# A hybrid decoder layer on one core: new order of the recurrence's levels, a steady weave with the output products, sixteen shared tiles, four PSUM banks in turn, and a weight column asked for sooner

## The chip, the core and the metric

The kernel runs on one core of one Trainium2 chip. A core has five engines that matter here: PE (TensorE, matrix products, with its weight loads shown as PEld), DVE (VectorE), ACT (ScalarE), POOL (GpSimd) and SP (SyncE, which here mostly starts transfers). Each engine executes its own instructions in order; semaphores tie the engines together. Data lies in HBM and is moved by DMA into SBUF (128 partitions); PE writes its sums into PSUM banks, from which ACT or DVE take them.

The metric is the device time of one execution in microseconds; the median of several runs is given.

## The reference

One layer of a decoder, 1024 tokens of width 1024 in float32, with 16 learned meta tokens ahead of them:

```python
h = h + 0.5 * swiglu(rms_norm(h, ffn1_norm[l]), ffn1_w_in[l], ffn1_w_out[l])
u = rms_norm(h, mix_norm[l]) @ w_in[l]
hq, hf, hi, hg, sq, sk, sv = jnp.split(u, ...)
o_hg = hgrn2(hq, hf, hi, hg, lb_all[l], hgrn_out_norm[l], valid)
o_sb = stick_breaking(sq, sk, sv, sb_q_norm[l], sb_k_norm[l], valid)
o = jnp.concatenate([o_hg, o_sb], axis=-1)
h = h + o @ w_out[l]
h = h + 0.5 * swiglu(rms_norm(h, ffn2_norm[l]), ffn2_w_in[l], ffn2_w_out[l])
```

The change lies in the middle: `hgrn2`, a gated linear recurrence of 4 heads (128 wide) over chunks of 128 tokens,

```python
bcum = jnp.cumsum(lf, axis=-2)
o_inter = jnp.einsum('bhtd,bhdv->bhtv', qk * jnp.exp(bcum), S)
attn = jnp.einsum('bhtd,bhsd,bhtsd->bhts', qk, kk, decay)      # decay = exp(bcum_t - bcum_s), causal
o_intra = jnp.einsum('bhts,bhsv->bhtv', attn, vk)
S_new = exp(b_last) * S + einsum('bhsd,bhsv->bhdv', kk * exp(b_last - bcum), vk)
```

then an RMS norm per head and a factor silu(g); `stick_breaking`, an attention of 8 heads; and the product with `w_out`.

## The kernel before

All large products are float32 by three products of split operands: a high part (rounded) and a low part of each side, `wh`, `wl` and `xh`, `xl`, added as xh·wh + xh·wl + xl·wh (lines 248 to 250). PE's instructions follow the order of the program text (`manual_schedule`), and that order is made by small planners: generators yield steps with a guess of their PE time in ns, and `weave` or `braid` deals them out. The other engines are ordered by a scheduler.

In order of time the layer is: the first feed-forward half (to about 760 us), the projections of the stick-breaking attention in four pairs of heads (`sb_project`, to about 843), the first of sixteen projected columns of the recurrence (`hgrn_fill`: v, f, q, g for each of 4 heads), the attention (`sb_jobs`) braided with these columns (to about 1160), the last columns beside the first steps of three heads, the recurrence (`hgrn_attend`) woven with the first half of the output product, `wo<-oT` (to 1293), the other half `wo<-oH` (to 1340), and the second feed-forward half.

**The passage from projections to attention.** `split_w` loads a column of weights (`raw`, 512 KB), casts its high part on ACT (line 231, kept as `self.rounded`) and takes the low part on DVE. `self.columns` is the list of columns asked for ahead; the last of it is the first column of the recurrence. `part` in `hgrn_fill` asks for column i+1 when column i begins. The pairs of `sb_project` end with `put_split`: q and k are scaled and split into `ohi` (ACT, line 1375) and `olo` (DVE, line 1376), in three buffers each, and stored to `qD` and `kD` by transfers that POOL starts (lines 1379 and 1380). For the last pair, p == 3, the splits are held behind `self.rounded` (line 1447), the newest cast at that time. The copies of the first projected column out of PSUM (`st`, line 1108) are held behind the cast of the column asked for last. The attention then loads `qs` and `ks`, makes its scores `z` (line 1599) and takes two sigmoids of each on ACT (`keep`, `sig`, lines 1605 and 1606).

**The recurrence.** `hgrn_attend` computes `attn` of a chunk level by level. After the diagonal (the `own` part, line 1199: products of KB and QA, masked with `ident` on DVE), each of the levels n = 1, 2, 4, ..., 64 takes: KP, a gathered copy of KB (ACT, line 1220); four products into a PSUM tile `lvl` (line 1225); the result put into `attn` (one `copy_predicated` on DVE up to n = 16, line 1232; copies on ACT above); then QA and KB are multiplied by the decays of the level (DVE, line 1255), which the next level reads. After the levels come the transposes of K (`knp`), the states (`s`, `up`), the outputs (`op`), their norm, a transpose (`onp`) and the split into `oH` (hi on ACT, lo on POOL). Before and between lie transposes of v (`flip`). Heads 0, 1 and 2 run as three streams, head 3 follows head 0.

PSUM has two banks for `lvl` (pool pz), two for `op` (po), two for small transposes (ptr) and two for projections.

`mix_out` is the output product: for each of 8 column blocks m and two halves of the tokens, four k steps of three products each; the first pass takes the attention's half of the rows (`oT`, k0 = 4), the second the recurrence's (`oH`, k0 = 0). `weave` runs a stream when its last step and the lag after it have passed, otherwise a step of the output product. The attention's result is read back from `oD` as `oT`, four tiles of 1 MB; the output weights come already split from `wout` in two buffers each.

## Time and profile before

| | |
|---|---|
| median of 3 runs | 1988.41 us (1987.54 to 1988.47) |
| the profiled execution | 1989.4 us |
| its span, first to last instruction | 1987.7 us |
| mean granted clock of TensorE | 0.998 |
| DVE, ACT, POOL busy | 1390.3, 854.7, 449.4 us |

The span is what the trace shows; the run's own time is 1.7 us longer, for what lies before the first and behind the last instruction. A row of a timeline gives start, duration, engine, line, operation, output and inputs, and in brackets how long the engine sat idle before it and what ended that. Lines with an L are those of the kernel before. One product of 4-byte operands shows as two records where it is 128 columns wide (a level's four products are eight records).

### The profile page before, as it was taken

How to read it: one execution, taken by the hardware profiler on the slowest of the kernel's cores; microseconds unless marked ns; L12 is line 12 of the kernel's file. 1: busy time of each engine (PE TensorE's matmuls, PEld its weight loads, DVE VectorE, ACT ScalarE, POOL GpSimd, SP SyncE). 2: the span in 40 equal slices, each digit the busy share in tenths (PEclk: the TensorE clock that was granted, in tenths of full speed). 3: DMA queues.
4: the chain of work that ended last, by engine and by line, in shares of the span. 5: the costliest groups of instructions: out<-in, count | busy, mean ns of one | idle time of the engine just before them, and what ended most of it. 6: DMA issues, size and time to landing. Idle time of an engine off the chain costs nothing.

```text
span 1987.7 us, 30439 instructions
## 1 busy us (share of the span) xinstructions
PE 1938.9 (98%) x10768; PEld 1631.7 (82%) x10768; DVE 1390.3 (70%) x2176; ACT 854.7 (43%) x1719; POOL 449.4 (23%) x616
## 2 busy tenths in 40 slices
PE   7999999999999999989999999899999999999998
PEld 6888888888888888878898978787888888888887
DVE  7977777877677765567777676567566766767774
ACT  6523443334444444456666635433233332344443
POOL 3010100010000003133333332220544544520000
PEclk9999999999999999999999999999999999999999
DMA  7366887758966225664454176665523323278463
GB/s 209 92 169 166 254 272 242 238 183 317 374 207 185 93 73 150 154 191 135 127 152 117 58 264 184 149 228 181 185 96 106 107 96 111 102 266 301 122 197 138
DMA packets 346168, 347.16 MB, mean 175 GB/s; under 512 B 94800, under 2 KB 250320, under 8 KB 346016
## 3 DMA queue, kind: packets, MB, share of 16 engines
q1 hardware_dynamic: 325168, 283.73, 46.5%
q0 software_dynamic: 19808, 61.49, 8.9%
q8 instruction: 85, 1.39, 0.3%
q14 instruction: 67, 0.55, 0.1%
q10 hardware_dynamic: 1040, 0.00, 0.0%
HBM read 233.75 MB, written 111.38 MB: 174 GB/s over the span
## 4 chain that ended last, share of the span: by engine, by line
PE 89%; DVE 4%; DMA 3%; ACT 2%; issue 1%; POOL 1%; SPq 0%; DVEq 0%; ACTq 0%; POOLq 0%
PE o L723 21%; PE qb L448 18%; PE qa L448 12%; PE qc L448 12%; PE proj L248 4%; PE proj L250 4%; PE proj L249 4%; PE flip L1454 2%; PE wo L248 1%; PE wo L249 1%; PE wo L250 1%; PE mq L992 1%; PE oacc L1529 1%; PE oacc L1531 1%; PE z L1599 1%
## 5 line engine op out<-in xcount | busy, mean ns | idle before, releaser
L448 PE MATMUL qb<-T,wh 128*128 128x512 f32 x1056 | 344.6, 390 | 1.4 <-ACT T L308 0.8
L448 PEld LDWEIGHTS qb<-T,wh 128*128 128x128 f32 x1056 | 198.1, 188 | 46.3 <-issue 2.5
L448 PE MATMUL qa<-B,wh 128*128 128x512 f32 x696 | 226.9, 391 | 0.0
L248 PE MATMUL proj<-xh,wh 128*128 128x512 f32 (+2 forms) x640 | 213.5, 334 | 2.6 <-ACT st L1108 1.5
L723 PE MATMUL o<-t,w 128*128 128x512 f32 x924 | 211.9, 390 | 0.5 <-DVE u L541 0.5
L250 PE MATMUL proj<-xl,wh 128*128 128x512 f32 (+2 forms) x640 | 209.8, 328 | 0.8 <-DVE xl L1918 0.8
L723 PE MATMUL o<-parts 128*128 128x512 f32 x924 | 209.9, 389 | 0.0
L249 PE MATMUL proj<-xh,wl 128*128 128x512 f32 (+2 forms) x640 | 209.7, 328 | 0.0
L448 PE MATMUL qb<-T,wl 128*128 128x512 f32 x528 | 205.4, 389 | 0.0
L723 PEld LDWEIGHTS o<-t,w 128*128 128x128 f32 x924 | 172.7, 188 | 37.4 <-issue 0.8
L723 PEld LDWEIGHTS o<-parts 128*128 128x128 f32 x924 | 173.3, 188 | 36.0
L361 DVE TENSOR_TENSOR wl<-s,wh 128x512 fp32r<-128x512 f32 x160 | 165.5, 1034 | 52.1 <-ACT wh L359 51.2
L359 ACT CAST wh<-s 128x512 fp32r<-128x512 f32 x160 | 99.4, 622 | 194.2 <-PE qb L448 150.7
L448 PEld LDWEIGHTS qa<-B,wh 128*128 128x128 f32 x696 | 130.8, 188 | 27.3 <-DVE B L827 0.3
L359 ACT CAST wh<-raw 128x512 fp32r<-128x512 f32 x120 | 74.4, 621 | 148.3 <-PE qc L448 106.6
L448 PE MATMUL qa<-B,wl 128*128 128x512 f32 x348 | 135.6, 390 | 0.0
L248 PEld LDWEIGHTS proj<-xh,wh 128*128 128x128 f32 x640 | 120.6, 188 | 14.7 <-ACT st L1108 1.7
L250 PEld LDWEIGHTS proj<-xl,wh 128*128 128x128 f32 x640 | 120.4, 188 | 12.2 <-DVE xl L1918 1.2
L249 PEld LDWEIGHTS proj<-xh,wl 128*128 128x128 f32 x640 | 120.5, 188 | 9.9
L448 PE MATMUL qc<-B,wh 128*128 128x512 f32 x352 | 115.0, 390 | 2.1 <-DVE u L541 2.1
L448 PE MATMUL qc<-T,wh 128*128 128x512 f32 x352 | 116.9, 394 | 0.0
L448 PEld LDWEIGHTS qb<-T,wl 128*128 128x128 f32 x528 | 99.1, 188 | 20.2
(398 smaller groups left out, 3871.8 us busy)
## 6 DMA issues: line engine op xcount, KB each, us to landing
raw<-in_ffn_w_in_dram SPq DMA_DIRECT2D x176, 256.0 KB, 4.0
raw<-in_ffn_w_out_dram SPq DMA_DIRECT2D x112, 256.0 KB, 4.3
w2in<-both SPq DMA_DIRECT2D x28, 512.0 KB, 3.4
raw<-in_w_in_dram SPq DMA_DIRECT2D x25, 512.0 KB, 4.8
ks<-kD SPq DMA_DIRECT2D x32, 260.0 KB, 5.0
wout<-both SPq DMA_DIRECT2D x16, 512.0 KB, 4.0
wh<-w2in SPq DMA_DIRECT2D x27, 256.0 KB, 3.2
wl<-w2in SPq DMA_DIRECT2D x27, 256.0 KB, 3.4
```

Of the source, the lines that this page charges most:

```text
L248: nc.tensor.matmul(ps, wh[:, s], xs, start=k == 0, stop=False)
L249: nc.tensor.matmul(ps, wl[:, s], xs, start=False, stop=False)
L250: nc.tensor.matmul(ps, wh[:, s], xl[:, k, c0 : c0 + n], start=False, stop=k == nk - 1)
L359: nc.scalar.copy(hi, src)
L361: nc.vector.tensor_sub(lo, src, hi.bitcast(F32))
L448: nc.tensor.matmul(ps, a[:, k, :], b[:, k, :], start=start and k == 0 and i == 0, stop=k == 3 and i == 2, skip_group_check=True,)
L723: nc.tensor.matmul(banks[bank][m], y[:, m * P : (m + 1) * P], z, start=start and at == 0 and e == 0, stop=q == nq - 1 and e == 2, skip_gro ...
L992: nc.tensor.matmul(ps[at : at + 32, at_g, :], self.xm[:, 4 * h + k, :], got[i, h][:, k, :], start=h == 0 and kk == 0, stop=h == 1 and kk = ...
L1454: self.nc.tensor.transpose(ps[:m, j, :], src[:, s0 : s0 + m], self.ident)
L1529: nc.tensor.matmul(o[:, c], vj, w[0], start=j == 0, stop=False, skip_group_check=True)
L1531: nc.tensor.matmul(o[:64, c], vj[:, :64], w[1], start=False, stop=end, skip_group_check=True)
L1599: nc.tensor.matmul(z, q, ks[0][:, s0 : s0 + n], start=True, stop=False)
```

## The change

Five things are changed.

1. The list of columns asked for ahead ends with the first two columns of the recurrence instead of one; the first column's turn may ask for one more. The splits of the last pair are held behind the cast of the second column instead of the newest one, and so are the copies of the first projected column.
2. A level multiplies KB by its decay right behind KP's copy, and QA right behind the products, ahead of `copy_predicated`. In the own part QA is multiplied ahead of the masking.
3. The tiles `lvl` and `op` take four PSUM banks in turn (`level_bank`: z and o alternate, two buffers each).
4. `weave` has a mode `steady`: a step of the output product comes whenever its share of planned time is behind that of the streams. The lags are changed (levels 6500 to 1500, own part 3200 to 1700, others), a step may carry a third number, its weight, and the last k steps are kept for the end.
5. `oT` is in 16 tiles of 128x512 (256 KB), eight for each half of the tokens, and their first asking comes behind the first weights; the last store of g is held behind them. The output weights of the second half use the same 16 slots (`w_tags`). Head 3's low part of oH is taken on DVE instead of POOL.

The diff, cut to its core:

```diff
+class Blocks:
+    def __init__(self, tiles):
+        self.tiles, self.shape = tiles, (P, len(tiles), 512)
+
+    def __getitem__(self, at):
+        rows, k, cols = at
+        return self.tiles[k][rows, cols]
...
+            for i, tag in enumerate(self.w_tags):
+                t = self.wp.tile([P, n], F32R, tag=tag, name="w" + "hl"[i], bufs=self.w_bufs)
+                self.last_load = nc.sync.dma_start(t.bitcast(F32), parts[:, i])
                 got.append(t)
             return got
...
                 nc.vector.tensor_mul(t, t, ps)
-            nc.sync.dma_start(dst[kind][h, :, s], t)
...
+            store = lambda: nc.sync.dma_start(dst[kind][h, :, s], t)
+            if (kind, h) == plan[-1] and c0 == HALVES[1][0]:
+                self.stores.append(store)
+            else:
+                store()
...
         def part(i, ci, c0, n, half):
             if ci == 0 and half == 0:
-                kept["w"] = kept["next"] or self.ahead_w.pop(cols[0])
-                kept["next"] = weights(i + 1) if i + 1 < len(plan) else None
-                kept["round"] = self.rounded.ins
+                kept["w"] = self.ahead_w.pop(cols[i])
+                for c in cols[i + 1 : i + (3 if i == 0 else 2)]:
+                    if c not in self.ahead_w:
+                        self.ahead_w[c] = self.col_tile(self.a["w_in"][0], c)
+                kept["round"] = self.rounds[cols[1]]
...
+    def level_bank(self, shape, name):
+        self.level_banks = self.level_banks[::-1]
+        tag = self.level_banks[0]
+        return (self.pz if tag == "z" else self.po).tile(shape, F32, tag=tag, name=name)
...
+        own = []
         for half in range(2):
-            ps = self.pz.tile([P, 4, P], F32, tag="z", name="lvl")
+            own.append(self.level_bank([P, 4, P], "lvl"))
             for j in range(4):
                 c = slice((4 * half + j) * P, (4 * half + j + 1) * P)
-                nc.tensor.matmul(ps[:, j, :], KB[:, c], QA[:, c], start=True, stop=True)
+                nc.tensor.matmul(own[half][:, j, :], KB[:, c], QA[:, c], start=True, stop=True)
+        nc.vector.tensor_mul(QA, QA, F)
+        for half, ps in enumerate(own):
             m = self.ident.unsqueeze(1).broadcast_to([P, 4, P])
             nc.vector.tensor_mul(attn[half], ps, m)
-        nc.vector.tensor_mul(QA, QA, F)
         tm = FM
...
-        yield 1740, 3200
...
-            ps = self.pz.tile([P, 2, 4, P // 2], F32, tag="z", name="lvl")
+            ps = self.level_bank([P, 2, 4, P // 2], "lvl")
             kp = pool.tile([P, 4 * P], F32, tag="KP", name="KP", bufs=2)
             nc.scalar.copy(
                 kp.rearrange("p (b h r) -> p b h r", h=2, r=n),
                 strided(KB, 0, (2 * n, 4 * nb), (512 + n, 2), (1, n)),
             )
+            decayed(KB, 0, 512 + n, 1, 8 * nb - 1)
             for c in range(4):
...
+            decayed(QA, n, 512 - n, 0, 8 * nb + 1)
             if n <= 16:
...
         for i, n in enumerate(LEVELS):
             level(i, n)
-            nb = 512 // (2 * n)
-            for eng, x, x0, x1, t0, t1 in (
-                (nc.vector, QA, n, 512 - n, 0, 2 * nb + 1),
-                (nc.vector, KB, 0, 512 + n, 1, 2 * nb - 1),
-            ):
-                y = strided(x, x0, (x1, 2), (2 * n, nb), (1, n))
-                eng.tensor_mul(y, y, strided(decays[i], t0, (t1, 2), (2, nb), (0, n)))
-            yield 890, 6500
+            yield 890, 1500, 2350 if n <= 16 else 1380
...
-        yield 1740, 4500
+        yield 1740, 2500, 5000 if last else 2800
...
-            ps = self.po.tile([P, 4, P], F32, tag="o", name="op")
+            ps = self.level_bank([P, 4, P], "op")
...
-            yield 1740, 3000
+            yield 1740, 3000, 9000 if last and half else 1740
...
+            eng = nc.vector if last else nc.gpsimd
+            eng.tensor_sub(lo[:, h, :], t, hi[:, h, :].bitcast(F32))
+            yield 430, 0, 2500 if last and half else 430
...
-            self.columns.append(self.columns_of_heads()[0])
+            self.columns += self.columns_of_heads()[:2]
...
-            with self.tc.issue_after(self.rounded.ins) if p == 3 else ExitStack():
+            with self.tc.issue_after(self.rounds[self.columns[-1]]) if p == 3 else ExitStack():
                 self.put_split(to, p, slice(c0, c0 + n), t[:, :n], mix, gain)
...
+                kept["w"] = ws.pop(m) if m in ws else self.rows_tile(k0, m)
+                if not k0:
+                    ws[m] = kept["w"]
...
-            self.product(ps, ws[m], *o[half], 0, n, [k])
+            self.product(ps, kept["w"], *o[half], 0, n, [k])
...
-    def weave(self, fill, streams=(), total=0.0, work=0.0, brief=False):
+    def weave(self, fill, streams=(), total=0.0, work=0.0, brief=False, steady=False):
...
             even = not work or spent * work <= (done + 6000) * total
-            if not ready and filling and join is None and (even or not live):
+            behind = steady and spent * work <= done * total
+            if filling and join is None and (behind or not ready and (even or not live)):
...
                 clock += step[0]
-                done += step[0]
+                done += step[-1] if len(step) == 3 else step[0]
...
                     def from_dram(half):
-                        got = []
-                        for i in range(2):
-                            t = self.pool_o.tile([P, 4, 512], F32R, name=f"oT{half}{i}")
-                            nc.sync.dma_start(
-                                t.bitcast(F32),
-                                oD[:, :, i, 512 * half : 512 * half + 512]
-                                .rearrange("k p t -> p k t"),
-                            )
-                            got.append(t)
-                        return got
+                        got = [[], []]
+                        for k in range(4):
+                            for i in range(2):
+                                t = self.pool_o.tile([P, 512], F32R, tag="o", name="oT", bufs=16)
+                                with tc.issue_after(self.last_load.ins) if half else ExitStack():
+                                    self.last_oT = nc.sync.dma_start(
+                                        t.bitcast(F32), oD[k, :, i, 512 * half : 512 * half + 512]
+                                    )
+                                got[i].append(t)
+                        return [Blocks(x) for x in got]
 
                     def first_half_of_o():
+                        ws = {0: self.rows_tile(4, 0)}
                         o = [from_dram(0)]
-                        yield 5000.0
+                        for store in self.stores:
+                            with tc.issue_after(self.last_oT.ins):
+                                store()
...
-                        self.weave(first_half_of_o(), lanes, 64 * 650.0 + 5000.0, 4 * 15900.0)
+                        self.weave(first_half_of_o(), lanes, 64 * 650.0 + 4000.0, 114850.0, steady=True)
...
-                    self.weights("wo2", 2, KT, c1)
+                    self.wp, self.w_tags, self.w_bufs = self.pool_o, ("o", "o"), 16
```

How this moves instructions, at three places. First ACT, around the splits of the last pair (`ohi`). Before, from the f column's sigmoids (L1114, L1115) on:

```order
L1114 ACTIVATE st<-proj 128x264
L1115 ACTIVATE st<-proj 128x264
L231 CAST wh<-raw 128x1024
L1375 ACTIVATE ohi<-qT,qg_82 128x512
L1114 ACTIVATE st<-proj 128x256
L1115 ACTIVATE st<-proj 128x256
L1375 ACTIVATE ohi<-qT,qg_82 128x512
L1114 ACTIVATE st<-proj 128x256
L1115 ACTIVATE st<-proj 128x256
L1375 ACTIVATE ohi<-kT,kg 128x512
L231 CAST wh<-raw 128x1024
L1375 ACTIVATE ohi<-kT,kg 128x528
```

and now, from the copies of the normalisation (`sbo`) on:

```order
L1455 COPY sbo<-sbs 32x65 x4
L1119 COPY st<-proj 128x264
L1459 ACTIVATE sbs<-sbs,eps 128x65
L1400 ACTIVATE ohi<-qT,qg_82 128x512
L1119 COPY st<-proj 128x256
L1400 ACTIVATE ohi<-qT,qg_82 128x512
L1400 ACTIVATE ohi<-kT,kg 128x512
L1119 COPY st<-proj 128x256
L1421 CAST vhl<-vt 128x32
L1400 ACTIVATE ohi<-kT,kg 128x528
L241 CAST wh<-raw 128x1024
L1125 ACT_TABLE_LOAD
```

Before, the splits stood behind the cast `wh` of a later column and among the f column's sigmoids; now all four stand ahead of that cast, of the table load and of the sigmoids.

Second PE, from the last projected column to the first output products. Before:

```order
L1225 MATMUL lvl<-QA,KP 128x2x64 x4
L1199 MATMUL lvl<-QA,KB 128x128 x8
L1454 MATMUL flip<-ident,vT 16x128
L1454 MATMUL flip<-ident,vT 128x128 x4
L1225 MATMUL lvl<-QA,KP 128x2x64 x2
L1454 MATMUL flip<-ident,vT 128x128 x4
L1225 MATMUL lvl<-QA,KP 128x2x64 x6
L1199 MATMUL lvl<-QA,KB 128x128 x8
L1225 MATMUL lvl<-QA,KP 128x2x64 x12
L248 MATMUL wo<-oT_12775,wh 128x512
L249 MATMUL wo<-oT_12775,wl 128x512
L250 MATMUL wo<-oT_12777,wh 128x512
```

and now:

```order
L1254 MATMUL lvl<-QA,KP 128x2x64 x4
L1219 MATMUL lvl<-QA,KB 128x128 x8
L1254 MATMUL lvl<-QA,KP 128x2x64 x4
L1479 MATMUL flip<-ident,vT 16x128
L1479 MATMUL flip<-ident,vT 128x128 x8
L1254 MATMUL lvl<-QA,KP 128x2x64 x4
L258 MATMUL wo<-oT,wh 128x512
L259 MATMUL wo<-oT,wl 128x512
L260 MATMUL wo<-oT,wh 128x512
L1254 MATMUL lvl<-QA,KP 128x2x64 x4
```

Before, six groups of levels and two own parts stood ahead of the first `wo`, which then ran 21 products at once; now three groups and one own part do, and behind the third group one or two k steps (of three products each) stand between any two levels. In all, from the last projection to the first product with `oH`, the output products stood in 25 runs before and stand in 42 now.

Third DVE, in the levels of three heads. Before:

```order
L1232 COPY_PREDICATED attn<-wide,lvl 128x2x64x4
L1255 TENSOR_TENSOR QA<-QA,Ts 128x2x64x4
L1255 TENSOR_TENSOR KB<-KB,Ts 128x2x64x4
L1232 COPY_PREDICATED attn<-wide,lvl 128x2x128x2
L1255 TENSOR_TENSOR QA<-QA,Ts 128x2x128x2
L1255 TENSOR_TENSOR KB<-KB,Ts 128x2x128x2
```

and now:

```order
L1241 TENSOR_TENSOR KB<-KB,Ts 128x2x32x8
L1241 TENSOR_TENSOR QA<-QA,Ts 128x2x128x2
L1262 COPY_PREDICATED attn<-wide,lvl 128x2x128x2
L1241 TENSOR_TENSOR KB<-KB,Ts 128x2x64x4
L1241 TENSOR_TENSOR QA<-QA,Ts 128x2x32x8
L1262 COPY_PREDICATED attn<-wide,lvl 128x2x32x8
```

Before, a level was copy, QA, KB; now KB of the coming level, QA of the one whose products have just run, and its copy behind them.

At the end of the recurrence two k steps stood between the last `op` and `onp`, and two behind; now four stand ahead of `onp`, and the products with `oH` follow it at once.

39 lines of the change are left out of this document (22 added, 17 removed).

## The prediction

> **What bounds the kernel now.** I read the page first, then busy time by stretch (windows), then the table of what PE waited for in each stretch, and last the timelines around those waits. The page's busy shares and the chain that ended last:
>
> ```profile
> PE 1938.9 (98%) x10768; PEld 1631.7 (82%) x10768; DVE 1390.3 (70%) x2176; ACT 854.7 (43%) x1719; POOL 449.4 (23%) x616
> PE 89%; DVE 4%; DMA 3%; ACT 2%; issue 1%; POOL 1%; SPq 0%; DVEq 0%; ACTq 0%; POOLq 0%
> ```
>
> PE is busy 1938.9 of 1987.7 us. The change takes no product away, so all it can win is PE's idle time, 48.8 us over the whole program, and time at a low clock. The windows of the places that the diff touches (stretch, length, then busy us and count of PE, PEld, DVE, ACT, POOL, then granted clock, DMA share, GB/s):
>
> ```profile
> 843.00:846.00 3.00, 1.51 (x13) 1.30 (x12) 1.29 (x3) 1.96 (x5) 1.63 (x2) 1.00 0.05 18
> 866.00:871.00 5.00, 0.00 (x0) 0.00 (x0) 2.00 (x2) 1.39 (x3) 0.54 (x1) 0.95 1.05 338
> 871.00:877.00 6.00, 5.17 (x14) 3.38 (x15) 4.49 (x6) 4.50 (x12) 3.14 (x9) 0.50 1.03 324
> 1162.00:1172.00 10.00, 9.32 (x61) 8.13 (x60) 5.30 (x8) 2.82 (x6) 8.58 (x25) 1.00 0.98 384
> 1170.50:1213.40 42.90, 37.87 (x252) 32.89 (x251) 40.76 (x61) 18.84 (x36) 12.87 (x30) 1.00 0.70 214
> 1213.40:1250.00 36.60, 35.14 (x260) 31.57 (x259) 21.61 (x49) 20.75 (x70) 12.05 (x20) 1.00 0.60 166
> 1250.00:1293.50 43.50, 38.97 (x235) 32.75 (x234) 21.23 (x39) 18.08 (x55) 11.97 (x12) 1.00 0.68 164
> ```
>
> The first three rows are the passage from the projections to the attention: PE does nothing from 866 to 871, and the six microseconds behind that run at a clock of 0.50. The last three are the recurrence beside the first half of the output product. PE idles 5.0, 1.5 and 4.5 us there, 11.0 together. In the first of them DVE is busy 40.76 of 42.90 us, in the other two only about half the time: its 83.6 us of work for these 123.0 us are crowded into the front. What PE waited for, in the passage and in the recurrence (us in total, times, longest; three rows of 0.4 us and less left off):
>
> ```profile
> PE z L1599 <- ACT sig L1606: 6.5, 4, 5.6
> PE proj L248 <- ACT st L1108: 1.5, 1, 1.5
> ```
>
> ```profile
> PE onp L1314 <- DVE vT L1308: 2.5, 2, 1.6
> PE lvl L1199 <- DVE attn L1232: 2.0, 3, 0.8
> PE lvl L1225 <- DVE QA L1255: 1.7, 3, 0.8
> PE lvl L1225 <- ACT KP L1220: 1.5, 2, 0.9
> PE wo L248 <- DMA wh<-wout: 1.1, 1, 1.1
> PE lvl L1225 <- DVE attn L1232: 0.9, 2, 0.5
> PE flip L1454 <- ACT vr L1188: 0.7, 1, 0.7
> PE lvl L1225 <- DVE attn L1201: 0.5, 1, 0.5
> ```
>
> The eight rows make 10.9 us, with the three left off 11.7 from 1160 on. Nothing else in the diff meets a wait of PE.
>
> **Part 1: the second column asked for sooner.** Why PE stood still, in the timelines of SP, POOL, ACT, DVE and PE (start, duration, instruction, idle before it and its releaser), and the transfer times of the first split stores of the pair before (tile ohi, 810 to 820) and of the last pair's (tile olo, 855 to 872):
>
> ```profile
> 831.39 0.62 SPq L226 DMA_DIRECT2D raw<-in_w_in_dram  x1
> 844.37 4.13 POOL L1438 TENSOR_TENSOR nat<-nat,sbs 128x512 f32<-128x512 f32 x4 [23.69 <-DVE sbs L1435]
> 853.89 1.28 ACT L1114 ACT_TABLE_LOAD   x1 [2.57 <-PE proj L250]
> 857.41 1.05 ACT L231 CAST wh<-raw 128x1024 fp32r<-128x1024 f32 x1
> 858.34 0.73 ACT L1375 ACTIVATE ohi<-qT,qg 128x512 fp32r<-128x512 f32 x1
> 870.21 0.77 DVE L1376 SCALAR_TENSOR_TENSOR olo<-kT,kg,ohi 128x528 fp32r<-128x528 f32 x1 [2.37 <-DMA qD<-olo]
> 871.07 0.29 ACT L1606 ACTIVATE sig<-z 128x144 f32<-128x144 f32 x1 [3.68 <-DVE olo L1376]
> 871.42 0.75 PE L1599 MATMUL z<-ks,qs 128*128 128x456 f32 x1 [5.58 <-ACT sig L1606]
> 877.46 0.39 PE L1454 MATMUL flip<-ident,sig 128*128 128x128 f32 x2
> DMA to landing us min/median/max: 2.8/4.1/6.1
> DMA to landing us min/median/max: 6.7/8.0/8.8
> ```
>
> The chain, backwards: z waits for ACT's sig, which stands in ACT's order behind the last split of k; its second half (olo, 870.21) waited for the landing of a qD<-olo store whose buffer it reuses. That store was slow (6.7 to 8.8 us, against 2.8 to 6.1 for a pair before) because the splits of the last pair ran at 858.34 and later, beside loads of the attention. And they ran there because L1447 holds them behind the cast of the newest column asked for, the one at 857.41.
>
> Now two columns are on the early list: the second is loaded right behind the first (near 822 by SP's listing, ten microseconds before 831.39), and the splits are held behind its cast. By ACT's order that cast stands right behind the copies of qT, so it runs near 838 (estimate from the ACT work listed ahead of it). The splits can then follow the normalised tiles, from about 848 (844.37 + 4.13 = 848.5 is the end of POOL's products), ten microseconds sooner and before the attention's loads. What this takes away: the 5.58 us gap; the 1.49 us wait of proj on ACT st (the 1.5 in the table), since the copies st stood behind the second column's cast and now do not; and the low clock in the burst of six z groups from 871.42 to 877.46 (6.0 us). At full clock this burst goes by ACT's pairs of keep and sig: 4.50 us of ACT work in the row 871 to 877, so I take 4.8 us, 1.2 less.
>
> What it adds: ACT has the four splits, the third column's cast and the table load now ahead of the first sigmoids, where the splits were behind them. The last splits need a buffer of which the store must land: first store about 850.2, landed 853.0 to 856.3 (2.8 to 6.1), then split 0.73, cast 1.05, table load 1.28, two sigmoids near 0.4 each: 856.9 to 860.2. PE, ahead by the 1.49 us, wants that PSUM bank from about 855. So a new wait of 1.9 us at the quick end, up to 5 at the slow one; I take 2.2, near the quick end, because these stores now meet little other traffic (the row 843 to 846 has a DMA share of 0.05). Sum of part 1: 1.49 + 5.58 + 1.2 - 2.2 = **6.1 us**, from 3.3 (new wait 5) to 8.3 (no new wait).
>
> The row 871 to 877 is what the Trainium skill describes in "TensorE: Matmul & The Clock Gate", section "HAM oscillation — how this bites in real kernels": an idle of some 3.4 us halves the clock. The trace agrees, with 5.58 us idle and then 0.50. By that rule a new wait above 3.4 us would halve the clock behind 855 too, so part 1 at its slow end would come to about 0 in place of 3.3.
>
> **Part 2: levels, banks and steady weave.** No product goes or comes; the prices of the pieces (DVE groups in 1160 to 1300; PE starts):
>
> ```profile
> L1232 DVE COPY_PREDICATED attn<-wide,lvl 128x512 f32<-128x512 uint8 x20 | 19.0, 952 | 10.6 <-PE lvl L1225 10.6
> L1255 DVE TENSOR_TENSOR QA<-QA,Ts 128x512 f32<-128x512 f32 x24 | 16.7, 696 | 5.8 <-PE lvl L1225 5.6
> L1255 DVE TENSOR_TENSOR KB<-KB,Ts 128x512 f32<-128x512 f32 x24 | 16.1, 687 | 0.8 <-ACT KP L1220 0.8
> 1170.53 1.07 PE L1225 MATMUL lvl<-QA,KP 128*128 128x128 f32 x8
> 1171.44 1.05 PE L1199 MATMUL lvl<-QA,KB 128*128 128x128 f32 x8
> 1184.97 0.48 PE L248 MATMUL wo<-oT,wh 128*128 128x512 f32 x1
> 1185.29 0.39 PE L249 MATMUL wo<-oT,wl 128*128 128x512 f32 x1
> 1185.52 0.40 PE L250 MATMUL wo<-oT,wh 128*128 128x512 f32 x1
> DMA to landing us min/median/max: 7.2/9.4/11.6
> ```
>
> A level of one head costs PE 0.91 us (1170.53 to 1171.44) and DVE 0.95 + 0.70 + 0.69 = 2.3. Before, levels of three heads stood behind each other and PE waited for DVE between them; 21 output products then ran at once. Now one or two k steps of wo (three products of 0.23, 0.69 us) stand between levels: 0.91 + 1.5 x 0.69 = 1.9 us of PE for 2.3 of DVE, instead of 0.91. The eight waits, one by one. The longest onp wait (1.6) has four wo steps, 2.8 us, ahead of it instead of two: gone, 0.4 of the 2.5 left. Own products behind attn, 2.0: four banks in turn instead of two, 0.5 left. QA, 1.7: its product now comes ahead of copy_predicated, but DVE still paces the levels, 1.0 left. KP, 1.5: KB's product no longer queues behind copy_predicated and QA on DVE, 0.5 left. The 1.4 behind attn: 0.5 left. flip and the rows left off, 0.7 + 0.8: 1.0 left. wo on DMA, 1.1: see below, 1.0 left. 11.7 becomes 4.9, a gain of 6.8. Against it: the first wo product behind small products takes 0.32 us to the next start (1184.97 to 1185.29) where the others take 0.23, so a switch costs 0.09; the listing has 42 runs of wo among the small products instead of 25, 17 x 0.09 = 1.5 us. Sum of part 2: 6.8 - 1.5 = **5.3 us**. At most 11.7 - 1.5 = 10.2; at the other end the 2.3 - 1.9 = 0.4 us by which DVE is short at each of the 20 levels with a copy_predicated comes back as waits, 8 us, which with 1.5 leaves 11.7 - 9.5 - 1.2 (the waits of wo and flip that stay) = 1.
>
> The tiles of oT: eight of 256 KB instead of two of 1 MB, all asked for once the first output weights are, behind the last proj (about 1170.7). 2.0 MB and 0.5 MB of weights at the 384 GB/s of row 1162 to 1172 take 6.8 us; the first k needs 1.0 MB, landed near 1175, the last near 1180. PE's new order has three level groups, an own group and nine flips (some 6 us) ahead of the first wo, and reaches the four k steps between 1177 and 1181: just in time, 0 to 2 us short, 1.0 taken above. Before, the first wo could start only at 1184.97.
>
> The Trainium skill speaks against such a split: "DMA: Bandwidth & Descriptors", section "Measured (HBM→SBUF, 128 partitions, SWDGE, issued from GpSimd)", has 1 MB as the size from which a transfer reaches three quarters of the peak, 64 KB at 32%. The row 1162 to 1172, with transfers of 256 and 512 KB queued behind each other, moves 384 GB/s and does not bear this out; by the page at, say, half the rate the last k would land near 1187, which is the late case among the rivals.
>
> At no cost: head 3's subtraction on DVE instead of POOL (0.69 by the QA row; nine output products, 2.1 us, run ahead of its reader), and the second set of output weights in oT's slots (half of it is loaded while half a pass of wo is left; the rest is asked for 11 us before its products, more than the 9.4 us in the landing row). Without that cover the first costs 0.7, the second 1 to 2.
>
> **Sum.** 1987.7 - 6.1 - 5.3 = 1976.3 us of span. The profiled run was 1989.4, its span 1987.7 and the median of the runs 1988.41, so a median stands 0.7 above a span: **1977.0**.
>
> **Rivals.** (a) Only part 1 pays; DVE paces the recurrence either way. For it: DVE's 40.76 of 42.90, and 2.3 against 1.9 per level. Against it: the slack of DVE behind 1213 into which the weave spreads it. 1988.4 - 6.1 = 1982.3. (b) Only part 2 pays: the wait moves to 855, 5 us long, and the clock halves there. For it: the row 871 to 877, and the 6.1 us at worst for a store. 1988.4 - 5.3 = 1983.1. (c) Slower: oT's tiles come late. They queue one behind the other, and the old ones took 7.2 to 11.6 us; PE executes in order, so a wo product waiting at 1177 holds every level behind it. It decides from a stall of about 5 us, the fourth k landing behind 1186: then 6 us idle, the clock at 0.50 for six more (3 us lost, as at 871), and 5.3 us of part 2 not won since DVE stands still meanwhile and is the pacing engine afterwards. 1988.4 - 6.1 + 6 + 3 = 1991.3. Against it: 384 GB/s in that row. (d) The change does not do what it says: the sooner load or cast finds no buffer and the splits stay late, and the levels keep their waits: 1988.4.
>
> **Chances.** Both parts pay: 0.62, and the time is that case's, 1977.0, with its own range 1970 (8.3 + 10.2) to 1983 (3.3 + 2.1). (a) 0.15, (b) 0.09, (c) 0.09, (d) 0.05. The range for 8 of 10 reaches over (a) and (b): 1969 to 1985.5. Of this kernel a measurement can tell 0.2%, 4 us, from no change, so faster means below 1984.4: all of the forecast's 0.62 but 0.01, 0.11 of (a) and 0.06 of (b), 0.78 in all. Same: 0.04 of (a), 0.03 of (b), 0.01 of the forecast, 0.01 of (c), 0.04 of (d), 0.13. Slower: 0.08 of (c), 0.01 of (d), 0.09.
>
> **What would show it.** Right in part 1: ohi on ACT near 848, the qD stores landing in under 6 us, no PE gap above 1 us between 860 and 880, clock 1.00 there, and one new PE wait near 855 on ACT st of about 2 us. Wrong: that wait above 3.4 us with a low clock behind it. Right in part 2: PE idle of about 5 us in the recurrence instead of 11.0, the first wo near 1177, DVE's busy share nearly even over its thirds, no onp wait above 0.5. Wrong: rows of lvl waiting for DVE that sum to more than 6 us, or wo waiting for oT. Anything that differs behind 1340, or before 800, is in no term here.

## The result

| | before | after |
|---|---|---|
| median of 6 runs | 1988.47 us (1987.54 to 1989.32) | 1974.95 us (1973.41 to 1976.45) |
| profiled execution, its span | 1989.4, 1987.7 us | 1973.63, 1971.9 us |
| mean granted clock | 0.998 | 0.999 |

The ratio after to before is 0.9932, 95% interval 0.9919 to 0.9945: 13.5 us faster, where the prediction's 1977.0 stood for 11.4. The two profiled executions lie on the far sides of their medians, so their spans differ by more, 15.8 us, and what follows from these two traces has to be read with that in mind. Where that came from, by the start of the same product in both traces:

| from ... to | before | after | won |
|---|---|---|---|
| start to the first projected product (`proj`) | 697.17 | 696.84 | 0.33 |
| ... to the first product of the attention's output (`oacc`) | 882.73 | 875.16 | 7.24 |
| ... to the last projection's first of three products | 1169.84 | 1161.24 | 1.03 |
| ... to the first product with `oH` | 1293.72 | 1278.46 | 6.66 |
| ... to the second feed-forward half's first product | 1340.01 | 1323.96 | 0.79 |
| ... to the last product | 1981.77 | 1965.82 | -0.10 |

Rows two and three are part 1 and what hangs on it, row four is part 2: the kernel with part 1 alone, among the experiments below, has 178.31, 286.08 and 123.79 us for the three stretches, where the kernel before has 185.56, 287.11 and 123.88. Row five is not explained in full: one wait of 0.33 us for a weight (`wl`) is gone, but the kernel with part 1 alone already has 45.69 of the 46.29 us there.

**The passage after.** What PE waited for from 840 to 885, and the windows of these microseconds (columns as before):

```profile
PE proj L258 <- ACT st L1126: 1.3, 1, 1.3
PE z L1624 <- ACT sig L1631: 1.1, 4, 0.5
```

```profile
843.00:846.00 3.00, 3.00 (x28) 3.00 (x27) 0.80 (x2) 1.51 (x6) 0.66 (x1) 1.00 0.86 162
846.00:853.00 7.00, 7.00 (x60) 7.00 (x60) 5.06 (x8) 3.57 (x8) 6.66 (x10) 1.00 0.39 137
853.00:857.00 4.00, 2.72 (x22) 2.51 (x21) 2.82 (x5) 3.15 (x5) 1.26 (x5) 1.00 0.95 336
857.00:864.00 7.00, 7.00 (x54) 6.65 (x53) 1.03 (x3) 1.99 (x4) 0.00 (x0) 1.00 0.76 228
864.00:871.00 7.00, 6.16 (x30) 4.02 (x29) 6.46 (x10) 6.73 (x21) 2.63 (x5) 1.00 0.68 188
```

The 8.0 us of waits of before are 2.4, PE works from 846 to 853 without a break, and the clock stays at 1.00. The one new wait of any size stands where it was expected. ACT ahead of it, PE behind it, and the transfer times of the last pair's stores (tiles ohi and olo, 845 to 870):

```profile
847.17 0.72 ACT L1400 ACTIVATE ohi<-qT,qg 128x512 fp32r<-128x512 f32 x1 [2.58 <-DVE qT L1469]
852.24 0.74 ACT L1400 ACTIVATE ohi<-kT,kg 128x528 fp32r<-128x528 f32 x1 [1.95 <-DMA qD<-ohi]
852.88 1.03 ACT L241 CAST wh<-raw 128x1024 fp32r<-128x1024 f32 x1
853.93 1.28 ACT L1125 ACT_TABLE_LOAD   x1
855.95 0.39 PE L258 MATMUL proj<-xh,wh 128*128 128x256 f32 x1 [1.28 <-ACT st L1126]
DMA to landing us min/median/max: 2.7/3.4/3.8
DMA to landing us min/median/max: 2.8/3.5/4.1
```

The first split runs at 847.17 instead of 858.34. The fourth waits 1.95 us for a store to land, then come the cast and the table load, and PE gets its bank 1.28 us late.

**The recurrence after.** What PE waited for from 1160 to 1280, and the windows of the recurrence:

```profile
PE knp L1290 <- DVE kms L1284: 1.6, 3, 0.6
PE wo L258 <- DMA oT<-oD: 0.9, 2, 0.5
PE lvl L1254 <- DVE QA L1220: 0.8, 1, 0.8
PE flip L1479 <- ACT vr L1207: 0.7, 1, 0.7
PE lvl L1254 <- DVE QA L1241: 0.6, 1, 0.6
PE flip L1479 <- DMA vT<-hg_v: 0.3, 1, 0.3
PE wo L260 <- DMA oT<-oD: 0.2, 1, 0.2
```

```profile
1161.90:1180.00 18.10, 16.36 (x106) 13.21 (x105) 17.24 (x25) 6.93 (x11) 10.87 (x29) 1.00 0.84 261
1180.00:1220.00 40.00, 38.97 (x268) 34.05 (x268) 27.60 (x54) 21.99 (x60) 8.80 (x16) 1.00 0.78 216
1220.00:1260.00 40.00, 37.72 (x253) 32.54 (x253) 28.76 (x50) 19.32 (x50) 10.76 (x13) 1.00 0.75 203
1260.00:1278.50 18.50, 18.50 (x122) 16.23 (x120) 7.69 (x19) 9.83 (x39) 5.03 (x5) 1.00 0.60 135
```

The waits make 5.1 us instead of 11.7. Those for attn, KP and onp are gone altogether. DVE is still full in the first 18 us (17.24 of 18.10); behind them it is busy 69%, 72% and 42%. By equal thirds of the recurrence DVE is busy 86%, 67% and 56%, where it was 94%, 64% and 46%.

### The profile page after: what moved, and what is told of

Read it like the earlier page. It is cut to its first block, busy times and chain, and to the rows that moved or that the text cites. A ratio compares the mean times of both kernels' runs of the same rounds, so it can differ in the third digit from the quotient of the medians.

```text
span 1971.9 us, 30437 instructions
## 1 busy us (share of the span) xinstructions
PE 1936.1 (98%) x10768; PEld 1629.3 (83%) x10768; DVE 1390.4 (71%) x2178; ACT 854.9 (43%) x1719; POOL 445.0 (23%) x614
## 4 chain that ended last, share of the span: by engine, by line
PE 73%; issue 16%; DVE 4%; DMA 2%; POOL 2%; ACT 2%; SPq 1%; POOLq 0%; DVEq 0%; ACTq 0%
PE o L733 21%; PE qb L458 11%; PE qa L458 8%; PE qc L458 7%; PE proj L258 4%; PE proj L260 4%; PE proj L259 4%; PE flip L1479 2%; PE wo L259 1%; PE wo L258 1%; PE wo L260 1%; PE oacc L1554 1%; PE oacc L1556 1%; PE z L1624 1%; DMA KB<-hg_k 1%
```

## The experiments

In the diffs the changed kernel (or, where said, the kernel before) is the minus side. Times are medians; the changed kernel has 1974.95. The cost in the trace is a stretch's length less that of the changed kernel: for the passage from the first projected product to the first `oacc` (178.32 us there), for the recurrence from the last projection to the first product with `oH` (117.22 us). Each trace is one execution. The five kernels that differ from the changed one in part 1 alone, with the recurrence untouched, have 116.34 to 117.90 us for the recurrence, so less than about 1.5 us there means nothing by itself. The kernel before was measured again with each set of experiments, at 1989.06 to 1989.50 us, and the ratios are to that set's own.

### The passage

**Part 1 undone, and part 1 alone.** Undone:

```diff
-            self.columns += self.columns_of_heads()[:2]
+            self.columns.append(self.columns_of_heads()[0])
-            with self.tc.issue_after(self.rounds[self.columns[-1]]) if p == 3 else ExitStack():
+            with self.tc.issue_after(self.rounded.ins) if p == 3 else ExitStack():
-                kept["round"] = self.rounds[cols[1]]
+                kept["round"] = self.rounded.ins
...
```

> The changed kernel with part 1 undone: one recurrence column on the early list, the splits of the last pair held behind the newest cast, the copies of the first projected column behind the second column's cast. My theory: the two parts are independent, so this gives back what the passage won in the traces, some 7.2 us (1.49 + 5.58 and the low clock behind, less the new wait of 1.3): about 1982, with PE idle from about 866 to 871 and a granted clock of 0.50 behind. Rival (part 2 carries the gain, and the passage only moved a wait): below 1978.

Measured 1981.79 us (ratio to before 0.9962, 0.9949 to 0.9975); the passage costs 6.90 us more, with 5.0 us of waits at the scores and a clock of 0.50 from 868 on. The other way round, these lines put into the kernel before:

> The kernel before with part 1 alone. My theory: 7 to 8 us faster than before, about 1981, and the wait of 5.58 us absent while the recurrence from 1160 on idles as before (about 11 us). Rival (the parts need each other): within 4 us of before.

1980.62 us (0.9961, 0.9946 to 0.9975). The passage is as in the changed kernel (178.31 us), the recurrence as before (123.79 against 123.88). So the two parts add up, and neither needs the other.

**What in part 1 does it.** Three kernels separate the hold on the splits from the earlier column. First only the hold put back:

```diff
-            with self.tc.issue_after(self.rounds[self.columns[-1]]) if p == 3 else ExitStack():
+            with self.tc.issue_after(self.rounded.ins) if p == 3 else ExitStack():
```

> The changed kernel, second column still early, but the splits of the last pair held again behind the newest cast (now the third column's, at about 853 in the profile of the changed kernel). My theory says the hold decides, not the time at which the column is loaded: the splits start 5 to 6 us later, near 853 to 856, their stores meet the attention's loads again, and 3 to 6 us of the 7.2 are given back: 1978 to 1981, with the copies st still free of their wait of 1.5. Rival (the earlier load and cast themselves are what counts): 1975, no gap before the scores.

1974.76 us: the rival's value. But the run did not do what it was made for: with the second column early the third is asked for earlier too, its cast ran at 848.73, and the splits started at 849.68, 2.5 us later than in the changed kernel and not 10. It costs 1.40 us in the passage and tells nothing of late splits. Second, the column late, the splits held behind the first column's cast alone:

```diff
-            self.columns += self.columns_of_heads()[:2]
+            self.columns.append(self.columns_of_heads()[0])
-                kept["round"] = self.rounds[cols[1]]
+                kept["round"] = self.rounded.ins
...
```

> The changed kernel with the second column asked for late as before, but the splits of the last pair held only behind the first column's cast. My theory (the hold decides): the 5.58 us gap and the low clock stay away, only the wait of proj on ACT st of about 1.5 us comes back: about 1976.5. Rival (the early load is what counts): 1982, with the gap near 866.

1983.08 us (0.9973, 0.9961 to 0.9984); the passage costs 10.07 us more, against 6.90 for undoing the whole part. My 1976.5 was wrong, and the rival's 1982 comes near for another reason than the one it gave. The scores' gap did go, but what PE waited for from 840 to 885 shows a new one:

```profile
PE proj L258 <- ACT st L1119: 9.8, 1, 9.8
PE z L1625 <- ACT sig L1632: 1.2, 4, 0.5
```

The copies st of the first column are held behind the second column's cast, and that cast now stood behind the four splits in ACT's order. Third, therefore, both holds put behind the first cast:

```diff
-            self.columns += self.columns_of_heads()[:2]
+            self.columns.append(self.columns_of_heads()[0])
-                kept["round"] = self.rounds[cols[1]]
+                kept["round"] = self.rounds[cols[0]]
...
```

> The changed kernel with the second column asked for late as before, and with both holds (the splits of the last pair, the copies st of the first projected column) put behind the first column's cast alone. In the run before this one, where st stayed held behind the second cast, the scores' gap of 5.58 us went away but the cast, now behind the splits in ACT's order, kept PE waiting 9.8 us for st. My theory (early splits are what frees the scores; the early column only serves to release the holds): no gap above 1 us at the scores, no wait for st, at most a wait of 1 to 2 us for the second column's late cast when its products begin: 1975 to 1977. Rival (the column itself has to come early): above 1980.

1980.62 us (0.9958, 0.9944 to 0.9972): my theory fell, and the median is on the rival's side of 1980. The waits of PE from 840 to 885, and ACT's timeline:

```profile
PE proj L258 <- ACT wh L241: 4.1, 1, 4.1
PE proj L259 <- DVE wl L243: 1.5, 1, 1.5
PE z L1625 <- ACT sig L1632: 1.1, 4, 0.5
```

```profile
851.76 0.73 ACT L1401 ACTIVATE ohi<-kT,kg 128x528 fp32r<-128x528 f32 x1 [2.00 <-DMA qD<-ohi]
852.40 0.35 ACT L1119 COPY st<-proj 128x256 f32<-128x256 f32 x1
852.66 1.04 ACT L241 CAST wh<-raw 128x1024 fp32r<-128x1024 f32 x1
```

With the splits early and nothing held behind the second cast, that cast itself is what comes late: it runs at 852.66 behind a split that waited for a store, and PE stood 4.1 us until it was done and another 1.5 for the low part (on DVE). The early column is not only there to release a hold; it moves this cast to 837.81, ahead of all splits.

Last, the column early but the splits late, as they were before:

```diff
-            with self.tc.issue_after(self.rounds[self.columns[-1]]) if p == 3 else ExitStack():
+            with self.tc.issue_after(self.rounded.ins) if p == 3 else ExitStack():
...
-                for c in cols[i + 1 : i + (3 if i == 0 else 2)]:
+                for c in cols[i + 1 : i + 2]:
```

> The changed kernel with the second column early, but the third asked for one turn later, as before, and the splits of the last pair held behind the third's cast: ACT's order of casts and splits is the one before. My theory: the splits run near 855 to 865 again, their stores take 6 us and more beside the attention's loads, and PE stands 3 to 6 us at the scores with the clock at 0.50 behind; only the wait of 1.5 us for st stays away: 1979 to 1981. Rival (the early second column is enough, by moving its load out of the crowd): 1975.

1977.32 us (0.9944, 0.9929 to 0.9959), under the range that I gave, though the mechanism is there. The splits run from 858.04, their stores take 4.6 to 7.2 us, and PE stands at the scores; windows, then PE's row:

```profile
864.00:867.20 3.20, 0.00 (x0) 0.00 (x0) 1.18 (x2) 0.91 (x4) 0.63 (x2) 1.00 1.00 370
867.20:868.00 0.80, 0.75 (x2) 0.35 (x2) 0.21 (x1) 0.57 (x2) 0.62 (x4) 0.65 1.05 382
868.00:869.00 1.00, 1.00 (x4) 0.57 (x3) 0.85 (x2) 0.60 (x2) 0.54 (x3) 0.50 1.04 393
867.25 0.60 PE L1624 MATMUL z<-ks,qs 128*128 128x456 f32 x1 [3.36 <-ACT sig L1631]
```

It costs 3.65 us in the passage. So of the passage's gain of 7.24 us about half needs the splits early (3.65 lost without), and early splits without the early cast lose most of it (6.06). The early column alone keeps 3.6 us, the early splits alone 1.2; only the two together give 7.2.

### The recurrence

**One item taken back at a time.** The old order in a level:

```diff
...
-            decayed(KB, 0, 512 + n, 1, 8 * nb - 1)
             for c in range(4):
...
-            decayed(QA, n, 512 - n, 0, 8 * nb + 1)
             if n <= 16:
                 nc.vector.copy_predicated(
...
                 )
+                decayed(QA, n, 512 - n, 0, 8 * nb + 1)
+                decayed(KB, 0, 512 + n, 1, 8 * nb - 1)
                 return
...
```

> The changed kernel with the old order inside a level alone: copy, then the products of QA and KB with the decay; own part masked before QA's product. My theory: KP of the next level waits again behind copy_predicated and QA on DVE, and PE's level products wait for KP and QA; the 3.2 us of these two rows in the profile before come back in part, 1 to 3 us: 1976 to 1978. Rival (the weave alone, by putting output products between levels, already hides this): within 0.5 us of the changed kernel.

1974.95 us (0.9930, 0.9915 to 0.9945), the same as the changed kernel; 0.40 us longer in the recurrence. The waits at the levels do come back: those for QA make 2.9 us instead of 1.4, and one for KP of 0.4 is there again. But the wait for oT (1.1) is gone and knp waits 0.9 instead of 1.6, so that the sum is 5.5 against 5.1. That PE, held up at a level, simply comes later to the next thing it would have waited for fits this, and is not tested further. Two banks for lvl and two for op:

```diff
-        self.level_banks = self.level_banks[::-1]
-        tag = self.level_banks[0]
+        tag = "z" if name == "lvl" else "o"
```

> The changed kernel with lvl in its own two PSUM banks and op in its own two, PE's order unchanged. My theory: PE waits again for attn (copy_predicated and the masking), the rows that made 3.4 us before and are gone now; 2 to 3 us back, 1977 to 1978. Rival (with output products between the levels a bank is always free in time): within 0.5 us.

1973.43 us (0.9925, 0.9910 to 0.9940), no change by the times. The profiled execution, at 1976.16 the slowest of its four (the others 1972.71 to 1973.69), has the waits that I expected. Its waits for attn from 1160 on, and windows at the two long ones (2.43 and 2.19 us) and behind them:

```profile
PE lvl L1218 <- DVE attn L1261: 4.6, 2, 2.4
PE lvl L1253 <- DVE attn L1261: 1.1, 2, 0.6
```

```profile
1163.20:1165.70 2.50, 0.10 (x1) 0.00 (x0) 2.50 (x3) 0.14 (x1) 2.34 (x6) 1.00 0.86 270
1165.70:1168.00 2.30, 2.27 (x13) 2.30 (x14) 1.20 (x2) 0.00 (x0) 1.52 (x9) 0.65 0.88 281
1168.00:1170.00 2.00, 1.94 (x10) 1.46 (x8) 2.00 (x4) 0.64 (x2) 0.00 (x0) 0.55 1.00 345
1227.40:1229.70 2.30, 0.11 (x2) 0.06 (x1) 2.14 (x5) 1.12 (x3) 0.00 (x0) 1.00 1.05 270
1229.70:1232.00 2.30, 2.30 (x16) 2.09 (x17) 2.19 (x4) 0.46 (x1) 0.00 (x0) 1.00 0.70 268
```

In that execution the recurrence is 3.16 us longer, and a part of it is a low clock behind the first wait. That the other three executions escaped the low clock would fit their times, and their mean granted clocks (0.999, 1.000 and 0.999 against 0.998); they have no trace, so it stays open.

The old weave (not steady, old lags, old weights of the steps):

```diff
-                        self.weave(first_half_of_o(), lanes, 64 * 650.0 + 4000.0, 114850.0, steady=True)
+                        self.weave(first_half_of_o(), lanes, 64 * 650.0 + 4000.0, 4 * 15900.0)
-            yield 890, 1500, 2350 if n <= 16 else 1380
+            yield 890, 6500
...
```

> The changed kernel with the old weave alone: not steady, old lags, so that levels stand behind each other (26 runs of output products instead of 42). My theory: DVE is crowded into the front again and PE idles 9 to 11 us in the recurrence instead of about 6, less 1.4 for the fewer switches: 3 to 4 us slower, 1978 to 1979. Rival (the level order and the four banks do the work, and the weave only adds switches): 1974.

1992.00 us (1.0014, 1.0005 to 1.0024): 17 us slower, over four times what I expected, and not by the mechanism that I named. Its largest waits from 1160 on:

```profile
PE wo L258 <- DMA wh<-wout: 7.1, 4, 3.7
PE onp L1338 <- DVE vT L1332: 5.8, 4, 1.9
```

Levels wait for DVE only 0.9 us there. With the old weave the output products come in bursts and outrun their weights, which stand in SP's queue behind eight tiles of oT each time: two of these loads, asked for at 1168.48 and 1188.99 behind such tiles, took 6.9 and 9.0 us to land, where the median of this kernel's loads of wh from 1160 to 1230 is 3.2, and PE went on at 1175.40 and 1198.06. The clock is at 0.88 from 1170 to 1213. At the heads' ends no product of the output stands between to cover onp. All waits from 1160 on make 18.3 us instead of 5.1, and PE's own work in the recurrence takes 118.5 us instead of 112.1, since a part of it runs at the low clock. So the old weave does badly with the new tiles. Which of its pieces (the mode, the lags, the weights) does it is not tested. Four tiles of 1 MB, PE's order kept:

```diff
-                                t = self.pool_o.tile([P, 512], F32R, tag="o", name="oT", bufs=16)
+                            t = self.pool_o.tile([P, 4, 512], F32R, name=f"oT{half}{i}")
...
-                    self.wp, self.w_tags, self.w_bufs = self.pool_o, ("o", "o"), 16
+                    self.weights("wo2", 2, KT, c1)
```

> The changed kernel with oT in four tiles of 1 MB instead of sixteen of 256 KB (and the last store of g ahead of them, the second weights in a pool of their own), PE's order unchanged. My theory: the first output product, at 1168.7 in the changed kernel, now needs two whole tiles of 1 MB, which took 7.2 and 9.2 us from issue before; PE stands still 4 to 6 us there, with a low clock for some microseconds behind: 1979 to 1983. Rival (large transfers move faster, so it comes out even): within 1 us of the changed kernel.

1979.58 us (0.9958, 0.9941 to 0.9974), as my theory had it. PE's two largest waits from 1160 on, the window behind the first, and the loads of oT:

```profile
PE wo L258 <- DMA oT<-oD: 4.5, 1, 4.5
PE wo L260 <- DMA oT<-oD: 1.6, 1, 1.6
1176.00:1178.00 2.00, 2.00 (x10) 1.94 (x9) 0.00 (x0) 0.00 (x0) 0.00 (x0) 0.50 0.00 0
DMA to landing us min/median/max: 6.5/7.0/7.4
```

They are asked for at 1166.00, 2.0 us later than the eight small ones, since a store of g and a second pair of weights stand ahead of them in SP's order, so a part of the 4.5 is that. The rest I put down to the first k step needing two whole megabytes; no run separates the two. Head 3's subtraction on DVE, also of this part, was not taken back by itself.

**Two against two.** The kernel before with part 1, the new level order and the four banks, without the weave and the tiles (minus side: the kernel before with part 1):

```diff
-            ps = self.pz.tile([P, 2, 4, P // 2], F32, tag="z", name="lvl")
+            ps = self.level_bank([P, 2, 4, P // 2], "lvl")
...
+            decayed(KB, 0, 512 + n, 1, 8 * nb - 1)
...
+            decayed(QA, n, 512 - n, 0, 8 * nb + 1)
             if n <= 16:
```

> The kernel before with part 1, the new order inside the levels and the four banks, but the old weave and oT in four tiles. It stands beside the kernel with part 1 alone (1980.6), the changed kernel (1975) and the next one. My theory after the runs so far (each of level order and banks taken back alone changed nothing measurable): the weave with the small tiles carries the gain of the recurrence, and this one gains 0 to 2 us on part 1 alone: 1978.5 to 1980.6. Rival (levels and banks give the gain whichever weave runs): 1975 to 1976.

Then the changed kernel with level order and banks both taken back:

```diff
-        tag = self.level_banks[0]
+        tag = "z" if name == "lvl" else "o"
...
-            decayed(KB, 0, 512 + n, 1, 8 * nb - 1)
...
-            decayed(QA, n, 512 - n, 0, 8 * nb + 1)
...
+                decayed(QA, n, 512 - n, 0, 8 * nb + 1)
+                decayed(KB, 0, 512 + n, 1, 8 * nb - 1)
```

> The changed kernel with the old order inside the levels and the two banks of lvl both taken back; steady weave, small tiles and part 1 stay. My theory: 1975 to 1978, that is at least half of the recurrence's gain is kept without the two. Rival (levels and banks stand in for each other, so that only both taken back show what they give): 1980 or more.

1977.96 us (0.9947, 0.9932 to 0.9962) and 1975.55 us (0.9932, 0.9917 to 0.9947). The recurrence in the four traces, with the last projection's and the first oH product's start:

| | neither | levels and banks | weave and tiles | both |
|---|---|---|---|---|
| starts | 1161.49, 1285.28 | 1161.77, 1282.80 | 1161.62, 1280.26 | 1161.24, 1278.46 |
| recurrence, us | 123.79 | 121.03 | 118.64 | 117.22 |
| median, us | 1980.62 | 1977.96 | 1975.55 | 1974.95 |

Levels and banks give 2.8 us where the old weave runs, against my 0 to 2, and 1.4 where the steady one does, which is within the spread of 116.34 to 117.90 named above; by the medians it is 0.6. Weave and tiles give 5.2 alone. The two gains overlap, 2.8 + 5.2 against 6.6 for both, but the pairs mostly remove different waits. With only levels and banks those for KP and onp stay, and most of those for attn (2.8 of 3.4 us; three rows of the list are shown), while QA falls from 1.7 to 0.5:

```profile
PE onp L1323 <- DVE vT L1317: 2.7, 2, 1.6
PE lvl L1240 <- DVE attn L1209: 2.2, 2, 1.7
PE lvl L1240 <- ACT KP L1234: 1.5, 2, 0.9
```

and with only weave and tiles KP and onp are gone, and waits for attn and QA remain (a row of 0.8 us for attn is left off):

```profile
PE lvl L1218 <- DVE attn L1259: 1.8, 2, 1.0
PE lvl L1252 <- DVE QA L1240: 1.2, 2, 0.7
PE lvl L1252 <- DVE QA L1222: 1.2, 1, 1.2
```

Weave and tiles make a second pair of this kind, each with part 1, the new level order and the four banks: neither 1977.96 us, the weave alone 1979.58, the tiles alone 1992.00, both 1974.95 (head 3's subtraction is on DVE in all but the first). Alone, the tiles cost 14 us and the weave gains nothing.

## Why the prediction was right, point by point

**Right in direction and size.** 1977.0 against 1974.95. The terms below are set against one trace of each kernel; these lie 15.8 us apart and the medians 13.5, so that a difference of a microsecond or two in a term is within what one execution can make. Of the 15.95 us in the table of stretches, 2.15 (0.33, 1.03 and 0.79) lie where the prediction had no term. Its slow end of the range took 2.1 us for part 2 where its own working gave 1; nothing hung on that.

**Part 1, 6.1 us predicted, 7.24 measured.** The gap of 5.58 us at the scores and the wait of 1.49 us for st went. The burst of z groups took 865.12 to 869.88, 4.8 us as estimated. The new wait was 1.28 us, below my quick end of 1.9: the first store left at 849.42 instead of 850.2 and landed in 2.7 us. That is 0.9 of the 1.14 us by which the term was too small. The chain named was right as to the hold and the collision of the stores (the run with late splits shows it), but incomplete: I had the early column as the means to an early hold, and the run with both holds behind the first cast shows 4.1 + 1.5 us of wait for the column's own cast. Another 1.03 us came in the attention behind, where one wait of flip for DVE shrank from 1.29 us to 0.38; I had no term for it. It goes with the time of the splits: that stretch takes 287.0 to 287.1 us in the three kernels whose splits start at 857 or later (the one before among them), and 285.95 to 286.17 us in the other eleven.

**Part 2, 5.3 us predicted, 6.66 measured.** The waits left are 5.1 us where I had 4.9. One by one: onp none (0.4 expected), own and attn none (0.5 + 0.5), KP none (0.5), QA 1.4 (1.0), wo on oT 1.1 (1.0), flip and the small rows 2.6 (1.0; knp's wait for kms grew from 0.2 to 1.6). That the sum came out within 0.2 is partly luck: rows that came out smaller by 1.9 us and rows that came out larger by 2.1 cancel. The first wo started at 1168.68, which is 1177.3 in the time of before, 8.6 us having been won ahead of it: where the order put it, and oT was 0.2 to 0.5 us short each time.

**The step that failed: the price of a switch.** I took 17 x 0.09 = 1.5 us for the more frequent changes between small and wide products, by the first wide product. The timeline of the changed kernel:

```profile
1181.30 1.05 PE L1254 MATMUL lvl<-QA,KP 128*128 128x128 f32 x8
1182.11 0.48 PE L258 MATMUL wo<-oT,wh 128*128 128x512 f32 x1
1182.42 0.40 PE L259 MATMUL wo<-oT,wl 128*128 128x512 f32 x1
1182.65 0.39 PE L260 MATMUL wo<-oT,wh 128*128 128x512 f32 x1
```

The first wide product does take 0.31 us to the next start where the next takes 0.23. But the eight small ones ahead of it take 0.81 us to its start, where eight small ones ahead of another small one took 0.91 (1170.53 to 1171.44 before). Over the recurrence the median of the 42 first wide products is 0.31 us and that of 23 levels ahead of a wide product 0.81. What one side loses the other gains: a switch costs nothing that these traces show, and 6.66 is the 11.7 - 5.1 = 6.6 of the waits alone. PE's busy time there did not rise with the 42 runs of output products: 112.1 us, against 112.9 before.

**Right number, edits partly wrong.** I credited the KP and QA terms to the new order inside a level and the attn terms to the banks. Taken back alone, neither moved the time. The waits show what each does. KP is the weave's: with weave and tiles alone it is gone, and with the old order under the steady weave only 0.4 us of it come back. QA and attn were credited to the right edits: QA comes back to 2.9 us with the old order, and attn to 5.7 in the one trace with two banks. But with output products between the levels the time hardly feels it: level order and banks together give 0.6 us by the medians there. DVE's share did not become even either, as I had forecast (86%, 67% and 56% by thirds): its first 18 us are as full as before, and what changed there is that PE has products to do meanwhile.

**The rivals.** Only part 1, or only part 2, paying was refuted by the kernel with part 1 alone and the one with part 1 undone. The late oT was no danger as built, but its mechanism is real: with 1 MB tiles, asked for 2.0 us later, PE stood 4.5 + 1.6 us and the clock fell to 0.50, and that gave back 4.6 of the 13.5 us.

## What to carry to other kernels

Follow a late transfer back through the order of the engine that feeds it: here a store was slow because a split was late because a cast of something else stood ahead, and moving only one of cast and split gave half of the gain at most. Where two streams share an in-order engine, put the filler between the steps of the stalling one rather than in blocks, and ask for its operands in pieces of the size in which it uses them; one of the two without the other was 5 or 17 us worse here, and no better than neither. When several edits can hide each other's waits, undo them in pairs as well as alone, and compare the lists of waits and not only the times, before giving any of them the credit.

## What the runs showed of the hardware

The clock can fall after a shorter idle than I had taken. The seven gaps of PE from 3.36 to 9.8 us in these traces all went with a granted clock of 0.50, in the gap or right behind it, and in the two-bank run one of 2.43 us was followed by 0.65 and 0.55 (in the windows above), while one of 2.19 us in the same execution left it at 1.00. The length of one gap does not decide alone: in the old-weave run one of 1.94 us (until 1175.40) was followed by three microseconds at 0.50, from 1177.4 on. What else decides, these traces do not show. The Trainium skill ("TensorE: Matmul & The Clock Gate", section "HAM oscillation — how this bites in real kernels") warns of gaps above some 3.4 us; these two runs show shorter ones.

On the size of transfers the Trainium skill ("DMA: Bandwidth & Descriptors", section "Measured (HBM→SBUF, 128 partitions, SWDGE, issued from GpSimd)") asks for 1 MB and more. Here the tiles of oT's first half landed 4.3 to 6.9 us after their issue at 256 KB and 6.5 to 7.4 us at 1 MB, and the kernel with the large tiles was the slower one by 4.6 us. A part of that is the 2.0 us by which its tiles were asked for later; the other that I see is that each product can start with the small piece that it reads.
